# Row skewness on one core: the closing of seven blocks and the last block's row sums on GpSimd, other last pieces, five square buffers

## The chip, the cores and the metric

The kernel runs on one core of one Trainium2 chip. The metric is the device time of one execution in microseconds (us), as the median of several runs.

## The reference

```python
def reference(x):                       # x: 1024 x 8192, float32
    mean = np.mean(x, axis=-1, keepdims=True)
    std = np.std(x, axis=-1, keepdims=True)
    z = (x - mean) / (std + 1e-8)
    return np.mean(z ** 3, axis=-1).astype(np.float32)
```

It gives the skewness of each row. With the raw moments m1, m2 and m3 of a row (the means of x, x^2 and x^3), the variance is m2 - m1^2, and the result is (m3 - 3 m1 (var + m1^2/3)) var^-1.5. The kernel computes it in this form, so x is read once.

## The kernel before, in words

The 1024 rows are eight blocks of 128: row 8p + b lies in partition p of block b. A block's 8192 columns are loaded in pieces whose widths the table UNITS lists, from 4096 columns in blocks 0 and 1 down to 512 at the end of block 7 (L is 7, the last block). All loads are issued by SyncE in this order (L129) into a pool of eight x buffers; a load waits until the piece eight places earlier has been used by ScalarE, VectorE and TensorE. The schedule is manual: each engine runs its instructions in the order in which the code writes them.

Each piece goes through three engines:

- TensorE transposes it in chunks of 128 columns against the identity, all of a block's chunks accumulating into one PSUM tile `tp` (L133). At the end of a block ScalarE copies `tp` to `tsb` (L163, in the last block L139), and a matmul with a column of 1/8192 makes the row means m1 in one column of the PSUM tile `s1ps` (L164).
- ScalarE squares the piece, or slices of it where it is wide (L145), scaled so that the accumulator gives the slice's part of m2. The part goes into a column of `s2u`, K columns to a block.
- VectorE multiplies the square by x (L149), in place, and its accumulator gives the slice's part of m3 in a column of `s3u`. In this document this is "the cube" of a piece.

The squares lie in a pool of four SBUF buffers up to piece 4 of block 6, and from piece 5 of block 6 on (PSUM_FROM) in two PSUM buffers called `psq`. A square therefore waits for the cube two pieces earlier, and a cube for the square of its own piece.

After piece 2 of block 7 (EARLY_AT) the blocks 0 to 6 are closed while loads go on. ScalarE copies the seven means to `m1a` (L156), VectorE sums the K columns of every block with two reductions (L107), ScalarE makes three small tiles out of `m1a` (L112 to L114), and GpSimd does the rest in six instructions of 128 x 7, one of them a power of -1.5 (L116 to L121).

In the last block, ScalarE sums the first five parts of m2 after the fifth piece (L160). In the last piece the copy to `tsb` (L139) stands ahead of the last square. Behind it: two GpSimd additions finish m2 (L171, L172), ScalarE squares the mean (`m1sq`, L173) and makes -3 m1 (L176), GpSimd makes `var` (L174) and its power (`rr`, L175), ScalarE makes v3 = m1^2/3 + var (L177), sums all but the last part of m3 (n3, L180) and makes num = v3 (-3 m1) + n3 (L181). One VectorE instruction ends the block (L182), and one store writes all results (L186).

Of the kernel before, what the change touches and what calls it, by code (L numbers as in the profile page):

```python
# [9 lines left out]
AF = mybir.ActivationFunctionType  # L10
ALU = mybir.AluOpType
X_AXIS = mybir.AxisListType.X
# [7 lines left out]
    [2944, 2688, 2560],  # L20
    [1920, 1920, 1792, 1536, 1024],
    [1536, 1408, 1408, 1152, 1408, 1280],
    [1152, 1280, 1408, 1280, 1280, 1280, 512],
]
PSUM_FROM = (6, 5)
SUB_MAX = 2304
PS_MAX, PS_BUFS = 1536, 2
X_BUFS = 8
SQ_BUFS = 4
EARLY = 7  # L30
EARLY_AT = (7, 2)


def _slices(w, most):
# [5 lines left out]
def _plan(b, k):  # L40
    return _slices(UNITS[b][k], PS_MAX if (b, k) >= PSUM_FROM else SUB_MAX)


@with_exitstack
def kernel(
    ctx: ExitStack,
    tc: tile.TileContext,
    x: bass.AP,
    out: bass.AP,
):  # L50
    nc = tc.nc
    eng = mybir.EngineType
    ctx.enter_context(tc.manual_schedule(
        engines={eng.PE, eng.Activation, eng.DVE, eng.Pool, eng.SP}))
    P = nc.NUM_PARTITIONS
    R, C = x.shape
    NB = R // P
    L = NB - 1
    F = EARLY
    inv_n = 1.0 / float(C)  # L60
    s_scale = float(C) ** -0.5
    third = (1.0 / 3.0) ** 0.5
    assert len(UNITS) == NB and all(sum(u) == C for u in UNITS) and F == L


    xv = x.rearrange("(p b) c -> b p c", b=NB)
    ov = out.rearrange("(p b) -> p b", b=NB)


    n_sl = [sum(len(_plan(b, k)) for k in range(len(u))) for b, u in enumerate(UNITS)]  # L70
    K = max(n_sl)

    xpool = ctx.enter_context(tc.tile_pool(name="xp", bufs=X_BUFS))
    sqpool = ctx.enter_context(tc.tile_pool(name="sqp", bufs=SQ_BUFS))
    onep = ctx.enter_context(tc.tile_pool(name="onep", bufs=1))
    psq = ctx.enter_context(tc.tile_pool(name="psq", bufs=PS_BUFS, space=bass.MemoryType.PSUM))
    psum1 = ctx.enter_context(tc.tile_pool(name="ps1", bufs=1, space=bass.MemoryType.PSUM))

    def small(name, n):
        return onep.tile([P, n], FP, tag=name, name=name)  # L80

    onesn = small("onesn", 1)
    nc.vector.memset(onesn, inv_n)  # L83
    tiny = small("tiny", 1)
    nc.scalar.activation(out=tiny, in_=onesn, func=AF.Square)  # L85
    ident = small("ident", P)
    make_identity(nc, ident)
    s2u = small("s2u", NB * K)
    s3u = small("s3u", NB * K)
    nc.vector.memset(s2u, 0.0)  # L90
    nc.vector.memset(s3u, 0.0)
    junk = small("junk", K)
    expo = small("expo", F)
    nc.gpsimd.memset(expo, -1.5)
    skew = small("skew", NB)
    m1a = small("m1a", F)
    tsb = small("tsb", P)

    tp = psum1.tile([P, P], FP, tag="tp", name="tp")
    s1ps = psum1.tile([P, NB], FP, tag="s1ps", name="s1ps")  # L100
    act, g = nc.scalar.activation, nc.gpsimd

    def close_first_blocks():

        m2, m3 = small("m2a", F), small("m3a", F)
        for dst, src in ((m2, s2u), (m3, s3u)):
            nc.vector.tensor_reduce(  # L107
                out=dst, in_=src[:, 0 : F * K].rearrange("p (b c) -> p b c", c=K),
                axis=X_AXIS, op=ALU.add,
            )  # L110
        m1sq, m1sq3, nm1 = small("m1sqa", F), small("m1sq3a", F), small("nm1a", F)
        act(out=m1sq, in_=m1a, func=AF.Square)  # L112
        act(out=m1sq3, in_=m1a, func=AF.Square, scale=third)
        act(out=nm1, in_=m1a, func=AF.Copy, scale=-3.0)  # L114
        var, rr = small("vara", F), small("rra", F)
        g.tensor_tensor(out=var, in0=m2, in1=m1sq, op=ALU.subtract)  # L116
        g.tensor_tensor(out=m1sq3, in0=m1sq3, in1=var, op=ALU.add)
        g.tensor_tensor(out=m1sq3, in0=m1sq3, in1=nm1, op=ALU.mult)
        g.tensor_tensor(out=m3, in0=m3, in1=m1sq3, op=ALU.add)
        g.tensor_tensor(out=rr, in0=var, in1=expo, op=ALU.pow)  # L120
        g.tensor_tensor(out=skew[:, 0:F], in0=m3, in1=rr, op=ALU.mult)  # L121

    for b, widths in enumerate(UNITS):
        c0 = 0
        j = b * K
        for k, w in enumerate(widths):
            last_unit = b == L and k == len(widths) - 1
            xt = xpool.tile([P, w], FP, tag="x", name=f"x_{b}_{k}")
            nc.sync.dma_start(out=xt, in_=xv[b, :, c0 : c0 + w])  # L129
            c0 += w  # L130
            n = w // P
            for c in range(n):
                nc.tensor.matmul(  # L133
                    out=tp, lhsT=xt[:, c * P : (c + 1) * P], rhs=ident,
                    start=(k == 0 and c == 0), stop=(c0 == C and c == n - 1),
                    is_transpose=True,
                )
            if last_unit:
                nc.scalar.copy(out=tsb, in_=tp)  # L139
            for s, e in _plan(b, k):  # L140
                if (b, k) >= PSUM_FROM:
                    sq = psq.tile([P, PS_MAX], FP, tag="psq", name=f"psq_{b}_{k}_{s}")[:, 0 : e - s]
                else:
                    sq = sqpool.tile([P, e - s], FP, tag="sq", name=f"sq_{b}_{k}_{s}")
                act(  # L145
                    out=sq, in_=xt[:, s:e], func=AF.Square, scale=s_scale,
                    accum_out=s2u[:, j : j + 1],
                )
                nc.vector.scalar_tensor_tensor(  # L149
                    out=sq,  # L150
                    in0=sq, scalar=1.0, in1=xt[:, s:e],
                    op0=ALU.mult, op1=ALU.mult, accum_out=s3u[:, j : j + 1],
                )
                j += 1
            if (b, k) == EARLY_AT:
                nc.scalar.copy(out=m1a, in_=s1ps[:, 0:F])  # L156
                close_first_blocks()
            if b == L and k == len(widths) - 3:
                m2p = small("m2p", 1)
                act(out=junk[:, 0 : n_sl[L] - 2], in_=s2u[:, L * K : j], func=AF.Copy,  # L160
                    accum_out=m2p)
        if b < L:
            nc.scalar.copy(out=tsb, in_=tp)  # L163
        nc.tensor.matmul(out=s1ps[:, b : b + 1], lhsT=tsb, rhs=onesn, start=True, stop=True)  # L164


    p1 = s1ps[:, L : L + 1]
    m1sq, nm1, v3, m2, var, rr, num = (
        small(f"{t}_l", 1) for t in ("m1sq", "nm1", "v3", "m2", "var", "rr", "num")
    )  # L170
    g.tensor_tensor(out=m2p, in0=m2p, in1=s2u[:, j - 2 : j - 1], op=ALU.add)  # L171
    g.tensor_tensor(out=m2, in0=m2p, in1=s2u[:, j - 1 : j], op=ALU.add)  # L172
    act(out=m1sq, in_=p1, func=AF.Square)  # L173
    g.tensor_tensor(out=var, in0=m2, in1=m1sq, op=ALU.subtract)  # L174
    g.tensor_tensor(out=rr, in0=var, in1=expo[:, 0:1], op=ALU.pow)  # L175
    act(out=nm1, in_=p1, func=AF.Copy, scale=-3.0)  # L176
    act(out=v3, in_=m1sq, func=AF.Identity, scale=1.0 / 3.0, bias=var)  # L177

    n3 = small("n3_l", 1)
    act(out=junk[:, 0 : n_sl[L] - 1], in_=s3u[:, L * K : j - 1], func=AF.Copy, accum_out=n3)  # L180
    act(out=num, in_=v3, func=AF.Identity, scale=nm1, bias=n3)  # L181
    nc.vector.tensor_scalar(  # L182
        out=skew[:, L:NB], in0=s3u[:, j - 1 : j], scalar1=num, scalar2=rr,
        op0=ALU.add, op1=ALU.mult,
    )
    nc.sync.dma_start(out=ov, in_=skew)  # L186
# [30 lines left out]
```

## Time and profile before

| | |
|---|---|
| median of 10 runs | 92.0 us (91.76 to 92.26) |
| the profiled execution's own time | 91.84 us |
| its span, first to last instruction | 90.0 us |
| VectorE busy | 73.9 us (82%) |
| ScalarE busy | 69.7 us (77%) |
| TensorE matmuls busy | 66.7 us (74%) |
| GpSimd busy | 4.4 us (5%) |
| loaded from memory | 33.55 MB |
| granted TensorE clock | 0.995 |

Busy shares are means over the whole span, while the end of the kernel is a chain of small dependent steps, so the table only says which engines are in use. What the change does is read from the timeline (each instruction with start, length, engine, line and shape; in brackets the idle time before it and what ended it), from the list of waits, and from the chain of work that ended last, which goes back from the last instruction to what released each step. The times of the views count from the start of the span.

### The profile page before, as it was taken

The page shows a single profiled execution, that of the slowest core. Times are in us where ns is not written, and L with a number is a line of the kernel's source. Part 1 is how long each engine was busy: PE and PEld are TensorE (multiplying, and loading weights), DVE is VectorE, ACT ScalarE, POOL GpSimd, SP SyncE. Part 2 cuts the span into 40 slices and gives each one's busy share as a digit, 9 for nine tenths or more (in the row PEclk, how much of TensorE's full clock was granted, in tenths as well). Part 3 has the DMA queues.
Part 4 walks back from the last instruction along what each step waited for, and adds up shares of the span by engine and source line. Part 5 has one row for each costly group of instructions (what it writes and reads, how often), then busy time and mean ns, then how long its engine had stood idle before and what let it go on. Part 6 is the DMA issues. An engine that isn't in the chain of part 4 may idle for free.

```text
span 90.0 us, 1444 instructions
## 1 busy us (share of the span) xinstructions
PE 66.7 (74%) x528; PEld 60.4 (67%) x528; DVE 73.9 (82%) x90; ACT 69.7 (77%) x106; POOL 4.4 (5%) x17
## 2 busy tenths in 40 slices
PE   0003999989886959898589779889798888897800
PEld 0003999979876949687569668878687677685700
DVE  0000498969999799999988999999999989989970
ACT  6003959589894979898589889989978889799950
POOL 3000000000000000000000000000000000004640
PEclk9999999999999999999999999999999999999997
DMA  4899999999999999999999999999999999994000
GB/s 116 342 393 451 437 451 393 437 459 407 425 394 450 427 424 400 453 419 415 417 438 400 417 430 427 406 411 407 417 413 414 417 417 412 414 406 187 0 0 2
DMA packets 4614, 33.64 MB, mean 374 GB/s; under 512 B 640, under 2 KB 640, under 8 KB 3072
## 3 DMA queue, kind: packets, MB, share of 16 engines
q1 hardware_dynamic: 4608, 33.56, 89.9%
q8 instruction: 4, 0.07, 0.3%
q14 instruction: 2, 0.02, 0.0%
HBM read 33.55 MB, written 0.00 MB: 373 GB/s over the span
## 4 chain that ended last, share of the span: by engine, by line
DMA 77%; ACT 8%; SPq 4%; PE 3%; issue 2%; DVE 2%; POOL 0%; DVEq 0%; POOLq 0%; ACTq 0%
DMA x<-in_x_dram 77%; ACT sq L145 6%; SPq L129 4%; PE tp L133 3%; DVE sq L149 2%; ACT psq L145 1%; ACT num_l L181 0%; ACT v_l L177 0%; DVE skew L182 0%; POOL var_l L174 0%; ACT junk L180 0%; POOL m_l L172 0%; ACT nm_l L176 0%; ACT m1sq_l L173 0%; DVEq L182 0%
## 5 line engine op out<-in xcount | busy, mean ns | idle before, releaser
L133 PE MATMUL tp<-ident,x 128*128 128x128 f32 x512 | 64.2, 283 | 15.6 <-DMA x<-in_x_dram 15.5
L149 DVE SCALAR_TENSOR_TENSOR sq<-sq,x 128x2048 f32<-128x2048 f32 (+9 forms) x34 | 62.0, 1873 | 12.3 <-ACT sq L145 12.2
L133 PEld LDWEIGHTS tp<-ident,x 128*128 128x128 f32 x512 | 58.5, 146 | 19.9 <-DMA x<-in_x_dram 11.5
L145 ACT ACTIVATE sq<-x 128x2048 f32<-128x2048 f32 (+9 forms) x34 | 53.5, 1576 | 14.0 <-DMA x<-in_x_dram 12.0
L149 DVE SCALAR_TENSOR_TENSOR psq<-psq,x 128x1280 f32<-128x1280 f32 (+3 forms) x8 | 11.0, 1409 | 0.3 <-ACT psq L145 0.2
L145 ACT ACTIVATE psq<-x 128x1280 f32<-128x1280 f32 (+3 forms) x8 | 9.3, 1161 | 0.7 <-DMA x<-in_x_dram 0.3
L145 ACT ACTIVATION_READ_ACCUMULATOR sq<-x 128x1 f32 x34 | 6.3, 185 | 0.0
L164 PEld LDWEIGHTS s1ps<-onesn,tsb 128*128 128x128 f32 x16 | 2.4, 188 | 5.3 <-ACT tsb L163 4.7
L164 PE MATMUL s1ps<-onesn,tsb 128*128 128x1 f32 x16 | 3.1, 261 | 3.4 <-ACT tsb L163 3.0
L116 POOL TENSOR_TENSOR vara<-m2a,m1sqa 128x7 f32<-128x7 f32 x1 | 0.2, 205 | 80.6 <-DVE m3a L107 80.6
L163 ACT COPY tsb<-tp 128x128 f32<-128x128 f32 x7 | 1.7, 250 | 1.4 <-PE tp L133 1.3
L149 DVE DVE_READ_ACCUMULATOR sq<-sq,x 128x1 f32 x34 | 2.8, 82 | 0.0
L85 ACT ACT_TABLE_LOAD x1 | 1.3, 1283 | 0.7 <-PEq L201 0.7
L120 POOL TENSOR_TENSOR rra<-vara,expo 128x7 f32<-128x7 f32 x1 | 1.5, 1506 | 0.0
L145 ACT ACTIVATION_READ_ACCUMULATOR psq<-x 128x1 f32 x8 | 1.5, 187 | 0.0
L149 DVE DVE_READ_ACCUMULATOR psq<-psq,x 128x1 f32 x8 | 1.1, 141 | 0.0
L83 DVE MEMSET onesn<- 128x1 f32 x1 | 0.1, 59 | 0.8 <-PEq L201 0.8
L177 ACT ACTIVATE v_l<-m1sq_l,var_l 128x1 f32<-128x1 f32 x1 | 0.3, 294 | 0.5 <-POOL var_l L174 0.5
L182 DVE TENSOR_SCALAR skew<-s3u,num_l,rr_l 128x1 f32<-128x1 f32 x1 | 0.3, 273 | 0.5 <-ACT num_l L181 0.5
L175 POOL TENSOR_TENSOR rr_l<-var_l,expo 128x1 f32<-128x1 f32 x1 | 0.6, 560 | 0.1
L139 ACT COPY tsb<-tp 128x128 f32<-128x128 f32 x1 | 0.3, 265 | 0.2 <-PE tp L133 0.2
L181 ACT ACTIVATE num_l<-v_l,n_l,nm_l 128x1 f32<-128x1 f32 x1 | 0.4, 387 | 0.0
(29 smaller groups left out, 5.0 us busy)
## 6 DMA issues: line engine op xcount, KB each, us to landing
x<-in_x_dram SPq DMA_DIRECT2D x4, 2048.0 KB, 14.1
x<-in_x_dram SPq DMA_DIRECT2D x4, 1472.0 KB, 27.1
x<-in_x_dram SPq DMA_DIRECT2D x5, 640.0 KB, 9.3
x<-in_x_dram SPq DMA_DIRECT2D x4, 704.0 KB, 10.1
x<-in_x_dram SPq DMA_DIRECT2D x2, 960.0 KB, 19.7
x<-in_x_dram SPq DMA_DIRECT2D x2, 896.0 KB, 22.5
x<-in_x_dram SPq DMA_DIRECT2D x1, 1728.0 KB, 25.3
x<-in_x_dram SPq DMA_DIRECT2D x2, 768.0 KB, 15.2
```

The source lines that it names most:

```text
L85: nc.scalar.activation(out=tiny, in_=onesn, func=AF.Square)
L120: g.tensor_tensor(out=rr, in0=var, in1=expo, op=ALU.pow)
L129: nc.sync.dma_start(out=xt, in_=xv[b, :, c0 : c0 + w])
L133: nc.tensor.matmul(out=tp, lhsT=xt[:, c * P : (c + 1) * P], rhs=ident, start=(k == 0 and c == 0), stop=(c0 == C and c == n - 1), is_transp ...
L139: nc.scalar.copy(out=tsb, in_=tp)
L145: act(out=sq, in_=xt[:, s:e], func=AF.Square, scale=s_scale, accum_out=s2u[:, j : j + 1],)
L149: nc.vector.scalar_tensor_tensor(out=sq, in0=sq, scalar=1.0, in1=xt[:, s:e], op0=ALU.mult, op1=ALU.mult, accum_out=s3u[:, j : j + 1],)
L163: nc.scalar.copy(out=tsb, in_=tp)
L164: nc.tensor.matmul(out=s1ps[:, b : b + 1], lhsT=tsb, rhs=onesn, start=True, stop=True)
L175: g.tensor_tensor(out=rr, in0=var, in1=expo[:, 0:1], op=ALU.pow)
L177: act(out=v3, in_=m1sq, func=AF.Identity, scale=1.0 / 3.0, bias=var)
L181: act(out=num, in_=v3, func=AF.Identity, scale=nm1, bias=n3)
```

## The change

- The pool of squares in SBUF has five buffers instead of four.
- Block 7 is loaded in pieces of 1280, 1408, 1408, 1408, 1152, 896 and 640 columns.
- The closing of blocks 0 to 6 comes after piece 0 of block 7 instead of piece 2, and is done by GpSimd except for the copy `m1a`. K is 8 instead of the largest number of slices (7), and each sum over a block's 8 columns is three additions in halves: 4 + 4, 2 + 2, 1 + 1. For s2u and s3u these are six instructions; nine others follow.
- In block 7, ScalarE's partial sum of m2 is gone. GpSimd sums the seven parts in four additions after the last square in the code.
- The copy to `tsb` of block 7 stands where that of every other block stands: behind the block's last square.

```diff
-    [1152, 1280, 1408, 1280, 1280, 1280, 512],
+    [1280, 1408, 1408, 1408, 1152, 896, 640],
...
-SQ_BUFS = 4
+SQ_BUFS = 5
 EARLY = 7
-EARLY_AT = (7, 2)
+EARLY_AT = (7, 0)
...
-    K = max(n_sl)
+    K = 8
...
+    def add(out, a, b):
+        g.tensor_tensor(out=out, in0=a, in1=b, op=ALU.add)
+
     def close_first_blocks():
         m2, m3 = small("m2a", F), small("m3a", F)
         for dst, src in ((m2, s2u), (m3, s3u)):
-            nc.vector.tensor_reduce(
-                out=dst, in_=src[:, 0 : F * K].rearrange("p (b c) -> p b c", c=K),
-                axis=X_AXIS, op=ALU.add,
-            )
-        m1sq, m1sq3, nm1 = small("m1sqa", F), small("m1sq3a", F), small("nm1a", F)
-        act(out=m1sq, in_=m1a, func=AF.Square)
-        act(out=m1sq3, in_=m1a, func=AF.Square, scale=third)
-        act(out=nm1, in_=m1a, func=AF.Copy, scale=-3.0)
-        var, rr = small("vara", F), small("rra", F)
+            v = src[:, 0 : F * K].rearrange("p (b c) -> p b c", c=K)
+            add(v[:, :, 0:4], v[:, :, 0:4], v[:, :, 4:8])
+            add(v[:, :, 0:2], v[:, :, 0:2], v[:, :, 2:4])
+            add(dst, v[:, :, 0], v[:, :, 1])
+        m1sq, t, var, rr = (small(n, F) for n in ("m1sqa", "ta", "vara", "rra"))
+        g.tensor_tensor(out=m1sq, in0=m1a, in1=m1a, op=ALU.mult)
         g.tensor_tensor(out=var, in0=m2, in1=m1sq, op=ALU.subtract)
-        g.tensor_tensor(out=m1sq3, in0=m1sq3, in1=var, op=ALU.add)
-        g.tensor_tensor(out=m1sq3, in0=m1sq3, in1=nm1, op=ALU.mult)
-        g.tensor_tensor(out=m3, in0=m3, in1=m1sq3, op=ALU.add)
         g.tensor_tensor(out=rr, in0=var, in1=expo, op=ALU.pow)
+        g.tensor_scalar(out=t, in0=m1sq, scalar1=1.0 / 3.0, scalar2=None, op0=ALU.mult)
+        g.tensor_tensor(out=t, in0=t, in1=var, op=ALU.add)
+        g.tensor_scalar(out=m1a, in0=m1a, scalar1=-3.0, scalar2=None, op0=ALU.mult)
+        g.tensor_tensor(out=t, in0=t, in1=m1a, op=ALU.mult)
+        g.tensor_tensor(out=m3, in0=m3, in1=t, op=ALU.add)
         g.tensor_tensor(out=skew[:, 0:F], in0=m3, in1=rr, op=ALU.mult)
...
-            if last_unit:
-                nc.scalar.copy(out=tsb, in_=tp)
             for s, e in _plan(b, k):
...
-            if b == L and k == len(widths) - 3:
-                m2p = small("m2p", 1)
-                act(out=junk[:, 0 : n_sl[L] - 2], in_=s2u[:, L * K : j], func=AF.Copy,
-                    accum_out=m2p)
-        if b < L:
-            nc.scalar.copy(out=tsb, in_=tp)
+        nc.scalar.copy(out=tsb, in_=tp)
         nc.tensor.matmul(out=s1ps[:, b : b + 1], lhsT=tsb, rhs=onesn, start=True, stop=True)
...
-    g.tensor_tensor(out=m2p, in0=m2p, in1=s2u[:, j - 2 : j - 1], op=ALU.add)
-    g.tensor_tensor(out=m2, in0=m2p, in1=s2u[:, j - 1 : j], op=ALU.add)
+    c = s2u[:, L * K : L * K + K]
+    add(c[:, 0:3], c[:, 0:3], c[:, 3:6])
+    add(c[:, 0:1], c[:, 0:1], c[:, 1:2])
+    add(c[:, 0:1], c[:, 0:1], c[:, 2:3])
+    add(m2, c[:, 0:1], c[:, 6:7])
```

More of the change, by code (lines that the diff above doesn't have):

```diff
@@ L61 @@
     s_scale = float(C) ** -0.5
-    third = (1.0 / 3.0) ** 0.5
     assert len(UNITS) == NB and all(sum(u) == C for u in UNITS) and F == L
@@ L70 @@
     n_sl = [sum(len(_plan(b, k)) for k in range(len(u))) for b, u in enumerate(UNITS)]
-    K = max(n_sl)
+    K = 8
+    assert max(n_sl) < K and n_sl[L] == 7
     xpool = ctx.enter_context(tc.tile_pool(name="xp", bufs=X_BUFS))
@@ L126 @@
         for k, w in enumerate(widths):
-            last_unit = b == L and k == len(widths) - 1
             xt = xpool.tile([P, w], FP, tag="x", name=f"x_{b}_{k}")
```

## The prediction

> **What bounds the kernel now.** I read three views in this order: the page's DMA row, the chain of work that ended last, and the timeline of the last 15 us. The DMA row and one issue row of the page:
>
> ```profile
> DMA  4899999999999999999999999999999999994000
> ...
> x<-in_x_dram SPq DMA_DIRECT2D x1, 256.0 KB, 8.4
> ```
>
> The DMA engines are full from slice 2 to 36, and even the last and smallest piece (512 columns) is issued 8.4 us before it lands: the load queue never runs dry, so landing times are set by bytes. The end of the chain (start, length, what):
>
> ```profile
> 73.53 9.62 DMA x<-in_x_dram
> 83.15 0.04 issue
> 83.19 1.76 PE tp L133 x14
> 84.95 0.02 issue
> 84.98 0.02 ACT tsb L139
> 85.00 0.14 issue
> 85.14 0.72 ACT psq L145 x2
> 85.86 0.06 ACT m1sq_l L173
> ```
>
> So the end is last landings, then PE, then ScalarE: `tsb` (L139) stands ahead of the last square and starts 0.04 after PE ends. Now the timeline, the last landings as PE sees them (it starts some 0.04 after a landing), the hand-over between ScalarE and VectorE, and the tail:
>
> ```profile
> 75.26 1.49 DVE L149 SCALAR_TENSOR_TENSOR psq<-psq,x 128x1280 f32<-128x1280 f32 x1
> ...
> 78.49 1.42 PE L133 MATMUL tp<-ident,x 128*128 128x128 f32 x11 [0.41 <-DMA x<-in_x_dram]
> 78.53 1.35 ACT L145 ACTIVATE psq<-x 128x1408 f32<-128x1408 f32 x1 [0.32 <-DMA x<-in_x_dram]
> ...
> 80.03 1.63 DVE L149 SCALAR_TENSOR_TENSOR psq<-psq,x 128x1408 f32<-128x1408 f32 x1 [0.23 <-ACT psq L145]
> 80.07 1.31 PE L133 MATMUL tp<-ident,x 128*128 128x128 f32 x10 [0.16 <-DMA x<-in_x_dram]
> ...
> 81.64 1.31 PE L133 MATMUL tp<-ident,x 128*128 128x128 f32 x10 [0.26 <-DMA x<-in_x_dram]
> ...
> 84.98 0.27 ACT L139 COPY tsb<-tp 128x128 f32<-128x128 f32 x1 [0.22 <-PE tp L133]
> 85.14 0.61 ACT L145 ACTIVATE psq<-x 128x512 f32<-128x512 f32 x1
> ...
> 85.30 0.38 PE L164 MATMUL s1ps<-onesn,tsb 128*128 128x1 f32 x2 [0.35 <-ACT tsb L139]
> 85.67 0.19 ACT L145 ACTIVATION_READ_ACCUMULATOR psq<-x 128x1 f32 x1
> 85.76 0.16 ACT L173 ACTIVATE m1sq_l<-s1ps 128x1 f32<-128x1 f32 x1
> ...
> 86.27 0.19 POOL L174 TENSOR_TENSOR var_l<-m_l,m1sq_l 128x1 f32<-128x1 f32 x1
> 86.50 0.29 ACT L177 ACTIVATE v_l<-m1sq_l,var_l 128x1 f32<-128x1 f32 x1 [0.51 <-POOL var_l L174]
> 87.49 0.27 DVE L182 TENSOR_SCALAR skew<-s3u,num_l,rr_l 128x1 f32<-128x1 f32 x1 [0.50 <-ACT num_l L181]
> ```
>
> What is to be seen: the transposed sum and the last square run at the same time today (PE has the sum at 85.68 while ScalarE squares until 85.75), and the square, not the sum, holds the row sum back.
>
> **What the Trainium skill says.** "PSUM — Partial Sum Buffer", section "Engine vs sequencer instructions": the ScalarE, VectorE and GpSimdE queues are strict FIFO, so a copy written behind a square can't pass it. The trace agrees: every ScalarE row comes in program order. "SBUF — State Buffer", section "Who interferes with whom": a VectorE instruction with two SBUF inputs contends with a GpSimd one that reads SBUF, one with a single SBUF input does not. The cubes of block 7 take psq from PSUM, and the trace agrees: a 1280 cube is followed by the next after 1.41 us with GpSimd idle (75.26 to 76.67) and after 1.41 with four GpSimd additions over it (81.81 to 83.22). "Perfetto Trace Analysis", section "GPSIMD Engine Instruction": go by start-to-start spacing, not by reported spans. Here the 7-element additions show 0.20 each and stand 0.28 apart; I use 0.28.
>
> **The change part by part.**
>
> *Five square buffers.* They end ScalarE's waits for VectorE in SBUF (1.7 us in four waits in the list of waits). The last is ahead of piece 4 of block 6, and gains 0.04. VectorE is back to back there and the loads are full anyway; nothing at the end. Cost nothing.
>
> *Closing on GpSimd, after piece 0 of block 7.* Gone are two VectorE reductions (81.58 to 81.81, 0.23), three ScalarE ones (80.08 to 80.39, 0.31) and the partial sum L160 (0.24). Added on GpSimd: 15 instructions, of them one power (1.51, from its row; 1.58 apart). The 28- and 14-element additions have no row; the page "GPSIMD Engine Reference", section 3.1, gives some 2.6 cycles an element, at 1.2 GHz an estimate of 0.05 for 21 elements more, so 0.33 is my value. Bounds: 0.28 (no element cost) and 1.5 (as dear as the power). s2u's three start by 75.2, s3u's follow the last cube of block 6 at 76.8; 76.8 + 3 x 0.33 + 8 x 0.28 + 1.58 = 81.6. Nothing asks for GpSimd before the last block's sums at 84.8: 3.2 us of cover. The copy `m1a` needs PE's sum of block 6 (75.86) and runs at 76.6, in ScalarE's wait for piece 1.
>
> *Last block in pieces 1280, 1408, 1408, 1408, 1152, 896, 640.* Landings: PE's starts 78.49, 80.07, 81.64 are 1280 columns apart, 1.575 each, or 1.23 ns a column; columns landed by then are 3840, 5120, 6400. So the new ends land at: piece 0 75.3, piece 1 (2688) 77.0, piece 2 (4096) 78.76, piece 3 (5504) 80.50, piece 4 (6656) 81.91, piece 5 by 83.0, piece 6 by 83.8. Hand-over times from the rows: a 1408 square's start to its cube's start 1.50 (78.53 to 80.03); cube start to next cube 1.55 for 1408, 1.41 for 1280, 1.32 for 1152 (76.67 to its accumulator read at 77.99); cube start to the square that reuses its PSUM buffer, two pieces on, 0.17 more (1.73 for 1408, 80.03 to 81.76; 1.49 for 1152). Interpolated between the 512 and 1408 rows, a square's accumulator read begins after 0.86 for 896 columns and 0.64 for 640, and a cube takes 1.04 for 896. With A for a square's start and D for a cube's:
> A2 = 78.76 + 0.05 = 78.81, D2 = 80.31. A3 = 80.55 (landing), D3 = 82.05 (D2 + 1.55 = 81.86 is earlier). D4 = D3 + 1.55 = 83.60. A5 = D3 + 1.73 = 83.78. D5 = D4 + 1.32 = 84.92. A6 = D4 + 1.49 = 85.09, today 85.14. The saved 0.23 of VectorE is thus spent on waiting for the larger pieces 1 to 3, and the last square starts where it did. Its accumulator read begins at 85.73.
>
> *`tsb` behind the last square, which the short description does not name.* PE is done by 84.6 (12 matmuls at 0.125 from piece 5's landing), but ScalarE reaches the copy only at 85.73 + 0.10 = 85.83, not 84.98. From copy to PE's end 0.70 (84.98 to 85.68), 0.04 to wake ScalarE: `m1sq` at 86.57, not 85.76. Then 0.16 for it and 0.06 for GpSimd to wake: `var` at 86.8 instead of 86.27. From there all rows are as before: 0.23 to v3, 0.99 to the last VectorE row: 88.02 against 87.49, **+0.53**.
>
> *Row sums of the last block on GpSimd.* Three additions wait for square 5 (read by 84.83) and are through by 85.7; the fourth waits for square 6 (85.92), starts at about 86.0 and ends at 86.2. That is 0.6 ahead of `var`'s other input: nothing. If GpSimd is late by more, the excess is added whole, since `var` and the power stand behind it. The power (87.07 to 87.63), the last cube (ends 86.9) and n3's inputs stay ahead of 88.02.
>
> Sum: +0.53. The profiled execution took 91.84 (span 90.0, 1.84 outside it), so its like would take 92.37; the median of ten is 92.0, 0.16 above it, hence 92.5.
>
> **The rivals.**
> *GpSimd late (slower still).* If the wide additions cost near 1.5, four of them add 4.7: the closing ends at 86.3, the four sums at 87.4 against 86.8: about +0.6 more, 93.1. For it: 4 such shapes have no row, and bigger operands made the power 1.51 instead of 0.56. Against: additions of 7 and of 1 element differ by 0.01.
> *Loads earlier (faster).* Piece 3's landing sets D3 to D6. If earlier buffer releases or larger pieces brought it forward by 0.87 or more, the cubes would run back to back from 75.26 (+ 1.41 + 1.41 + 3 x 1.55 = D4 at 82.73), and the end would come at 88.02 - 0.87 = 87.15: 0.34 before today's, 91.65. It decides from a landing 0.53 earlier on. For it: ScalarE runs ahead more freely. Against: DMA full, the same bytes, the queue 8 us deep.
> *No change that can be measured* (within 0.2%, 0.18 us, about what a measurement of this kernel can tell from no change): the same with 0.35 to 0.7 of it, 92.0. For it: wait times in a tail differ by some 0.1. Against: the 0.81 on the copy is program order.
>
> **How the numbers follow.** Forecast as worked out 0.75, within 92.3 to 92.75 since each of some five hand-overs is known to about 0.05; GpSimd late 0.12; no change 0.07; faster 0.06. Slower by over 0.2%: 0.87. Range 92.2 to 92.85: it leaves out faster, no change and the half of the late case.
>
> **What would show it.** Right: `tsb` on ScalarE behind the last square and 0.8 later; the last square within 0.1 of 85.14; `var` waiting for ScalarE's `m1sq`, not for a GpSimd sum; closing done by 82; VectorE waiting for squares in pieces 1 to 3; last row at 88.0. Wrong: `var` waiting behind GpSimd's own additions, or piece 3 landing before 80.

## The result and the profile after

The changed kernel takes **92.57 us** (median of 9 runs, 92.44 to 92.73) against 92.02 (32 runs): ratio 1.0060, 95% interval 1.0051 to 1.0069, slower by 0.55 us. 92.5 was forecast, slower with a chance of 0.87.

The profiled execution took 92.79 us, its span is 91.0. It is 0.22 above its kernel's median, where the profiled one of before was 0.18 below: 0.40 of the 0.95 between the two profiles is the choice of execution. It is seen in the loads. Piece 5 of block 6, to which the change does nothing, lets TensorE start at 74.09 instead of 73.76; in the traces of e1, e7 and e8 below, which are the same as the changed kernel up to there, the start is at 73.81 to 73.85. Where a time below is called *aligned*, this 0.33 is taken off.

From the DMA view of the changed kernel, the DMA row and the issue row of the last and smallest piece (now 640 columns):

```profile
DMA  4899999999999999999999999999999999991000
...
x<-in_x_dram SPq DMA_DIRECT2D x1, 320.0 KB, 8.3
```

The DMA engines are as full as before, and the last piece is again issued more than 8 us before it lands. The end of the chain of work that ended last (start, length, what):

```profile
85.45 0.03 ACT psq L144
85.47 0.62 issue
86.09 0.19 ACT psq L144
86.28 0.16 ACT tsb L157
86.44 0.04 issue
86.48 0.40 PE s1ps L158 x2
86.88 0.02 issue
86.90 0.17 ACT m1sq_l L170
```

Before, the copy to `tsb` stood between TensorE and the last square, and `m1sq` came right behind the square's accumulator read. Now the square comes first, then its read, then the copy, then the matmul, and only then `m1sq`: all in a row, where before the matmul ran beside the square. The timeline of the changed kernel:

```profile
78.95 1.63 DVE L148 SCALAR_TENSOR_TENSOR psq<-psq,x 128x1408 f32<-128x1408 f32 x1 [0.34 <-ACT psq L144]
...
80.68 1.63 DVE L148 SCALAR_TENSOR_TENSOR psq<-psq,x 128x1408 f32<-128x1408 f32 x1
...
80.87 4.04 PE L134 MATMUL tp<-ident,x 128*128 128x128 f32 x32 [0.31 <-DMA x<-in_x_dram]
...
82.41 1.63 DVE L148 SCALAR_TENSOR_TENSOR psq<-psq,x 128x1408 f32<-128x1408 f32 x1
...
85.45 0.71 ACT L144 ACTIVATE psq<-x 128x640 f32<-128x640 f32 x1 [0.27 <-DVE psq L148]
...
86.19 0.25 ACT L157 COPY tsb<-tp 128x128 f32<-128x128 f32 x1
...
86.42 0.19 POOL L104 TENSOR_TENSOR m_l<-s2u 128x1 f32<-128x1 f32 x1 [0.43 <-ACT tsb L157]
...
86.90 0.17 ACT L170 ACTIVATE m1sq_l<-s1ps 128x1 f32<-128x1 f32 x1 [0.47 <-PE s1ps L158]
...
87.22 0.19 POOL L171 TENSOR_TENSOR var_l<-m_l,m1sq_l 128x1 f32<-128x1 f32 x1 [0.60 <-ACT nm_l L173]
...
88.44 0.27 DVE L179 TENSOR_SCALAR skew<-s3u,num_l,rr_l 128x1 f32<-128x1 f32 x1 [1.20 <-ACT num_l L178]
```

To be read here: the sum in `tp` is ready at 84.91 (80.87 + 4.04), and the copy starts at 86.19, 1.28 later, while ScalarE is at the square of piece 5 until 85.18, waits 0.27 for VectorE to free a PSUM buffer, and then squares piece 6. The last m2 addition on GpSimd starts at 86.42 and ends at 86.61, long before `var` (87.22): the row sums on GpSimd are not what `var` waits for. VectorE waits for the wider pieces: the cubes of pieces 1, 2 and 3 start 1.73 apart (78.95, 80.68, 82.41), where the next one follows after 1.55 (83.96).

### The profile page after: what moved, and what is told of

Its sections match the earlier page's. It is cut to its first block, busy times and chain, and to the rows that moved or that the text cites. A ratio compares the mean times of both kernels' runs of the same rounds, so it can differ in the third digit from the quotient of the medians.

```text
span 91.0 us, 1445 instructions
## 1 busy us (share of the span) xinstructions
PE 66.8 (73%) x528; PEld 60.5 (67%) x528; DVE 73.7 (81%) x88; ACT 69.3 (76%) x101; POOL 6.8 (7%) x28
## 4 chain that ended last, share of the span: by engine, by line
DMA 67%; issue 9%; ACT 9%; DVE 8%; SPq 3%; PE 0%; POOL 0%; DVEq 0%; ACTq 0%
DMA x<-in_x_dram 67%; DVE sq L148 6%; ACT sq L144 6%; SPq L130 3%; ACT psq L144 2%; DVE psq L148 2%; PE s1ps L158 0%; ACT num_l L178 0%; ACT v_l L174 0%; DVE skew L179 0%; POOL var_l L171 0%; ACT junk L177 0%; ACT m1sq_l L170 0%; ACT tsb L157 0%; ACT nm_l L173 0%
## 5 line engine op out<-in xcount | busy, mean ns | idle before, releaser
L148 DVE SCALAR_TENSOR_TENSOR psq<-psq,x 128x1408 f32<-128x1408 f32 (+4 forms) x8 | 11.0, 1412 | 0.4 <-ACT psq L144 0.3
L144 ACT ACTIVATE psq<-x 128x1408 f32<-128x1408 f32 (+4 forms) x8 | 9.3, 1163 | 1.7 <-DMA x<-in_x_dram 0.9
L104 POOL TENSOR_TENSOR s2u<-s2u 128x1 f32<-128x1 f32 (+3 forms) x5 | 1.1, 211 | 78.0 <-ACT psq L144 77.8
L172 POOL TENSOR_TENSOR rr_l<-var_l,expo 128x1 f32<-128x1 f32 x1 | 0.6, 582 | 0.1
L104 POOL TENSOR_TENSOR s3u<-s3u 128x28 f32<-128x28 f32 (+1 forms) x2 | 0.5, 228 | 1.0 <-DVE psq L148 0.9
```

What stands on the lines that cost most here:

```text
L104: g.tensor_tensor(out=out, in0=a, in1=b, op=ALU.add)
L144: act(out=sq, in_=xt[:, s:e], func=AF.Square, scale=s_scale, accum_out=s2u[:, j : j + 1],)
L148: nc.vector.scalar_tensor_tensor(out=sq, in0=sq, scalar=1.0, in1=xt[:, s:e], op0=ALU.mult, op1=ALU.mult, accum_out=s3u[:, j : j + 1],)
```

## The experiments

All ratios are to the kernel before on the same chip, with 95% intervals. The runs are from several chips, on which the kernel before has medians from 91.92 to 92.02, so kernels are compared by their ratios.

| kernel | median us | ratio |
|---|---|---|
| changed kernel | 92.57 | 1.0060 (1.0051 to 1.0069) |
| e1: changed, copy ahead of the last square | 92.01 | 1.0009 (0.9997 to 1.0021) |
| e2: before, copy behind the last square | 92.20 | 1.0025 (1.0017 to 1.0034) |
| e3: before, five buffers | 91.97 | 1.0007 (0.9997 to 1.0018) |
| e4: before, new pieces | 92.16 | 1.0023 (1.0015 to 1.0030) |
| e5: before, closing on GpSimd | 91.92 | 1.0005 (0.9995 to 1.0014) |
| e6: before, row sums on GpSimd | 91.89 | 1.0001 (0.9994 to 1.0009) |
| e11: before, new pieces and copy behind | 92.67 | 1.0072 (1.0059 to 1.0084) |
| e8: changed, closing behind piece 4 | 93.81 | 1.0204 (1.0191 to 1.0217) |
| e9: changed, all squares in SBUF | 94.83 | 1.0317 (1.0297 to 1.0337) |
| e7: e1, last square in SBUF | 92.36 | 1.0039 (1.0025 to 1.0053) |
| e10: e1, three PSUM buffers, 1024-column pieces | 91.86 | 0.9982 (0.9974 to 0.9990) |
| e12: e10, copy behind the last square | 91.93 | 0.9999 (0.9990 to 1.0007) |

**e1, the copy's place undone.**

```diff
+            if b == L and k == len(widths) - 1:
+                nc.scalar.copy(out=tsb, in_=tp)
             for s, e in _plan(b, k):
...
-        nc.scalar.copy(out=tsb, in_=tp)
+        if b < L:
+            nc.scalar.copy(out=tsb, in_=tp)
```

> The changed kernel with one thing undone: in block 7 the copy to tsb stands ahead of the last square again. Theory (the copy behind the last square puts the matmul and m1sq on the path): m1sq comes right behind the last square's accumulator read, var at the pace of the last m2 addition, 0.54 earlier than in the changed kernel (87.22 there): 92.57 - 0.54 = 92.03 us, level with the kernel before. Rival A (GpSimd's row sums or closing hold the end): no gain, 92.5 to 92.6. Rival B (later landings of the larger pieces hold the end whatever stands on ScalarE): 92.4 to 92.6.

Measured 92.01, the theory's number: everything else of the change together can't be told from no change, and is at most 0.2%. The timeline of e1:

```profile
84.83 0.25 ACT L140 COPY tsb<-tp 128x128 f32<-128x128 f32 x1
...
85.93 0.15 ACT L173 ACTIVATE m1sq_l<-s1ps 128x1 f32<-128x1 f32 x1
...
86.43 0.19 POOL L174 TENSOR_TENSOR var_l<-m_l,m1sq_l 128x1 f32<-128x1 f32 x1
```

The copy starts at 84.83 instead of 86.19, `m1sq` at 85.93 directly behind the last square, and `var` comes at 86.43. In the changed kernel it was 87.22. The cube of piece 4 starts at 83.70 here and at 83.96 there, so 0.26 of the 0.79 between them is the loads, and 0.53 the copy's place. Both rivals fall.

**e2, e4 and e11: the copy's place and the pieces, alone and together, on the kernel before.**

```diff
-            if last_unit:
-                nc.scalar.copy(out=tsb, in_=tp)
...
-        if b < L:
-            nc.scalar.copy(out=tsb, in_=tp)
+        nc.scalar.copy(out=tsb, in_=tp)
```

is e2; e4 is the line of widths alone,

```diff
-    [1152, 1280, 1408, 1280, 1280, 1280, 512],
+    [1280, 1408, 1408, 1408, 1152, 896, 640],
```

and e11 is both.

> The kernel before with one thing of the change: the copy to tsb of block 7 behind the last square. There the last square (512 columns) stood behind the copy and can now start at 84.84 (the PSUM buffer of piece 4's cube) instead of 85.14, its read at 85.37, the copy at 85.46, m1sq at 86.20, var at 86.43 against 86.27. Theory (the position costs what is not won back by the earlier square): +0.16, 92.18 us. Rival A (the copy's position costs its full 0.53 whatever the pieces are): 92.55. Rival B (it costs nothing, the pieces or GpSimd do): 92.0.

> The kernel before with the new widths of block 7 only (the copy ahead of the last square, closing on VectorE and ScalarE as before). Theory: the small ScalarE closing steps delay square 3 to 80.7 and the two reductions stand behind cube 2, so cube 3 starts at 82.2, cube 4 at 83.75, the last square at 85.24 and var at 86.48 instead of 86.27: +0.2, 92.2 us. Rival A (pieces alone make the whole loss): 92.5. Rival B (pieces alone cost nothing): 92.0.

> The kernel before with two things of the change: the new widths of block 7 and the copy to tsb behind the last square (closing as before on VectorE, ScalarE and GpSimd). Alone they cost 0.2 each. Theory (with the wide pieces the last square can't start earlier when the copy is moved away, since it waits for cube 4's PSUM buffer at 85.24, so the copy's delay comes whole): read of the last square at 85.88, copy at 85.97, m1sq at 86.71, var at 87.0 against 86.27: +0.7, 92.7 us. Rival (the two costs only add): +0.4, 92.4 us.

Measured 92.20, 92.16 and 92.67; the theories had 92.18, 92.2 and 92.7. Alone, each costs 0.25% and 0.23%. Together they cost 0.72%, and not the 0.48% of a mere sum. The last square, in the timeline of e2,

```profile
84.92 0.60 ACT L143 ACTIVATE psq<-x 128x512 f32<-128x512 f32 x1
```

and in that of e11:

```profile
85.31 0.71 ACT L143 ACTIVATE psq<-x 128x640 f32<-128x640 f32 x1 [0.27 <-DVE psq L147]
```

With the old pieces the last square started at 85.14, behind the copy; with the copy gone from ahead of it, it starts at 84.92 in e2, as soon as the PSUM buffer of cube 4 is free (84.88), and so gives back part of the delay. With the new pieces that buffer comes free later, and the square waits for it in either case: until 85.31 in e11, where the bracket names VectorE, and until 85.23 in e4, though the copy is over at 85.10 there (84.86 + 0.24). The accumulator read of cube 4 ends at 85.19 in e4. Its timeline, the copy and the last square:

```profile
84.86 0.24 ACT L139 COPY tsb<-tp 128x128 f32<-128x128 f32 x1
...
85.23 0.71 ACT L145 ACTIVATE psq<-x 128x640 f32<-128x640 f32 x1
```

So nothing comes back when the copy is moved away.

**e3, e5 and e6: the three other parts, each alone on the kernel before.**

```diff
-SQ_BUFS = 4
+SQ_BUFS = 5
```

is e3. e5 takes the new `close_first_blocks` with EARLY_AT (7, 0) and K = 8, and e6 the four additions in place of L160, L171 and L172, both as the diff of the change has them.

> The kernel before with five SBUF buffers for squares. Theory (loads are full, VectorE is back to back where ScalarE waited): 92.0 us, within 0.1. Rival (buffers release x earlier and the load stream ends earlier, or the stream is disturbed): a time outside 91.9 to 92.15, with landings in block 7 moved by as much.

> The kernel before with the closing of blocks 0 to 6 as GpSimd instructions after piece 0 of block 7, K 8, everything else as before (pieces, tsb ahead of the last square, ScalarE's partial sum of m2). Theory: VectorE saves 0.23 and ScalarE 0.3, but the last square waits for the copy to tsb, and that for TensorE at 84.94, as before: 92.0 us, within 0.1. Rival A (GpSimd's closing slows VectorE or comes late): 92.2 or more. Rival B (the freed 0.23 reaches the end): 91.8.

> The kernel before with only the row sums of the last block as four GpSimd additions (L160's partial sum on ScalarE gone). Theory: the first three lie under the last two squares, the fourth waits for the last square as the addition before did: 92.0 us, within 0.1. Rival A (four additions in a row come late, each 0.28): up to 92.5. Rival B (ScalarE freed by 0.24 starts the squares earlier and gains): 91.8.

Measured 91.97, 91.92 and 91.89, each with 1 inside its interval. The copy to `tsb` in the timeline of e5:

```profile
84.90 0.27 ACT L141 COPY tsb<-tp 128x128 f32<-128x128 f32 x1 [0.27 <-PE tp L135]
```

It still waits for TensorE, and the last square stands behind it, so what VectorE and ScalarE save has nowhere to go, as the theory said. In e3 the fifth buffer wins ScalarE no time: its waits for VectorE among the SBUF squares (1.7 us in four in the kernel before) are gone from the list of waits, but those for VectorE and for loads together come to 14.0 us, against 13.7 before, and the idle times ahead of pieces 2 and 4 of block 6 are still 0.27 and 0.47, now ended by a landing. In the changed kernel's own list the waits for VectorE still stand, with 1.9 us in five.

**e8, GpSimd made late.**

```diff
-EARLY_AT = (7, 0)
+EARLY_AT = (7, 4)
```

> The changed kernel with the closing behind piece 4 of block 7 (the copy m1a comes at 83.6, so GpSimd's eight instructions behind it, 3.64 us in the changed kernel's trace, end at 87.4 instead of 81.66, and the four row sums follow). Theory (GpSimd is off the path in the changed kernel only because of its cover; when late, the excess is added whole): last row sum at 88.2, var at 88.5 instead of 87.22: +1.3, 93.9 us. Rival (row sums are already on the path in the changed kernel): the whole 5.7 us of shift appears, 98 us. Rival (GpSimd plays no part): 92.6.

Measured 93.81. The timeline of e8:

```profile
86.97 0.20 POOL L123 TENSOR_TENSOR skew<-m3a,rra 128x7 f32<-128x7 f32 x1
...
87.94 0.19 POOL L104 TENSOR_TENSOR m_l<-s2u 128x1 f32<-128x1 f32 x1
88.21 0.19 POOL L171 TENSOR_TENSOR var_l<-m_l,m1sq_l 128x1 f32<-128x1 f32 x1
```

Here the closing's last instruction runs at 86.97, and the last addition and `var` stand behind it on GpSimd without idle time. So the prediction's rival "GpSimd late" is a real mechanism with the price it was given, excess added whole; the changed kernel escapes it by its cover.

**e9, all squares in SBUF.**

```diff
-PSUM_FROM = (6, 5)
+PSUM_FROM = (8, 0)
```

> The changed kernel with all squares in SBUF (five buffers) and none in PSUM. Two things change: cubes have two SBUF inputs while GpSimd adds, and the last square no longer waits for the PSUM buffer of cube 4. Theory A (no contention to speak of, the PSUM buffer holds the last square, and with it the copy to tsb): last square at 84.4 instead of 85.45, var 1.05 earlier, end 1.0 earlier: 91.5 to 91.6 us. Theory B (as the Trainium skill's SBUF page says, GpSimd's reads contend with such cubes): cubes of pieces 0 to 3 over GpSimd's closing are longer than the 1.41 and 1.55 us of a free VectorE, and part of the gain is lost: 91.7 to 93.

Measured 94.83, above both expectations. The last square did start early (84.11), as theory A had it, and it did not matter. The contention of theory B is there, but not where I put it. The timeline of e9:

```profile
77.01 1.34 POOL L104 TENSOR_TENSOR m2a<-s2u 128x7 f32<-128x7 f32 x1
...
80.40 1.65 POOL L104 TENSOR_TENSOR m3a<-s3u 128x7 f32<-128x7 f32 x1
...
82.01 0.20 POOL L115 TENSOR_TENSOR m1sqa<-m1a 128x7 f32<-128x7 f32 x1
...
82.08 1.63 DVE L148 SCALAR_TENSOR_TENSOR sq<-sq,x 128x1408 f32<-128x1408 f32 x1
82.29 1.49 POOL L116 TENSOR_TENSOR vara<-m2a,m1sqa 128x7 f32<-128x7 f32 x1
```

`m2a` and `m3a` are additions of 7 elements (to a partition), which take 0.21 and 0.20 in the changed kernel; here their rows are 1.34 and 1.65 long. `m1sqa`, which starts at 82.01 in the gap between two cubes, takes 0.20, and the next one, of the same size, takes 1.49 and ends at 83.78, when the cube of 82.08 is over (83.71). The cubes hardly suffer: 1.63 for 1408 columns, as in the changed kernel. So VectorE keeps what it has and GpSimd waits for the end of the cube. The closing ends at 88.21 instead of 81.66, and the row sums come late as in e8.

**e7, only the last square in SBUF** (on e1), to take away its wait for cube 4 and to test e9's reading on one instruction.

```diff
-                if (b, k) >= PSUM_FROM:
+                if (b, k) >= PSUM_FROM and (b, k) != (7, 6):
```

> e1 (the changed kernel with the copy to tsb ahead of the last square), with the last square in SBUF, so that it does not wait for cube 4. Theory A (no contention): last square, m1sq and m2 0.2 earlier, 91.8 us. Theory B (a GpSimd addition that comes up while a cube with two SBUF inputs runs waits for that cube's end, as in e9): the last cube (from 86.1 to about 86.9) now has two SBUF inputs, and var stands behind it, at 86.9 instead of 86.43: 92.4 to 92.5 us.

Measured 92.36, next to theory B's 92.4 and far from theory A's 91.8. The timeline of e7:

```profile
86.08 0.82 DVE L150 SCALAR_TENSOR_TENSOR sq<-sq,x 128x640 f32<-128x640 f32 x1
86.23 0.72 POOL L174 TENSOR_TENSOR var_l<-m_l,m1sq_l 128x1 f32<-128x1 f32 x1
```

The square came 0.2 earlier, but `var` of one element, 0.19 long in e1, comes up 0.15 into a cube with two SBUF inputs and ends with it (86.95 against 86.90).

**e10 and e12, a version against the tail's own limits.** e10, on e1:

```diff
-    [1280, 1408, 1408, 1408, 1152, 896, 640],
+    [1024, 1024, 1024, 1024, 1024, 1024, 1024, 640, 384],
...
-PSUM_FROM = (6, 5)
+PSUM_FROM = (7, 0)
...
-PS_MAX, PS_BUFS = 1536, 2
+PS_MAX, PS_BUFS = 1024, 3
...
-    add(m2, c[:, 0:1], c[:, 6:7])
+    add(c[:, 0:1], c[:, 0:1], c[:, 6:7])
+    add(c[:, 0:1], c[:, 0:1], c[:, 7:8])
+    add(m2, c[:, 0:1], c[:, 8:9])
```

s2u and s3u get one more column for the ninth piece.

> e1 with block 7 in pieces of 1024 x 7, 640 and 384 columns, its squares in three PSUM buffers of 1024 columns in place of two of 1536 (piece 5 of block 6 in SBUF), and two more row-sum additions. Theory (the tail is the last landing plus one hand-over for each engine; two buffers of wide pieces make the last square wait for a cube two pieces back): squares start at their landings, the last one at about 84.3, m1sq at 85.1, var at 85.4, n3 behind cube 7 at 86.2, last row near 87.0 instead of 88.44 in the changed kernel: 91.1 to 91.3 us. Rival (more pieces cost VectorE and ScalarE as much as the hand-over saves, or landings hold the end): 91.9 to 92.2.

Measured 91.86, ratio 0.9982 with an interval below 1: faster than both kernels, but than the kernel before by only some 0.15 us where I expected 0.8. The squares of pieces 3 to 6 do start at their landings, 0.03 to 0.04 after TensorE. What I had wrong is TensorE. Its timeline from piece 6's landing on:

```profile
82.93 1.97 PE L134 MATMUL tp<-ident,x 128*128 128x128 f32 x16
```

It has the 16 matmuls of the last three pieces to do, 0.123 each, and never waits among them: piece 6 alone keeps it until 83.9. It ends at 84.90, and an earlier landing of the last two pieces would not change that. The expectation had the last square at about 84.3, so the copy and TensorE's sum ahead of that. The copy starts at 84.98, and the last square behind it at 85.15.

> e10 (1024-column pieces, three PSUM buffers) with the copy to tsb behind the last square, as the changed kernel has it. In e10's trace ScalarE is free and the buffer is free at 84.76, while TensorE's sum ends at 84.9 and the copy starts at 84.98. Theory (the position costs only what the earlier start of the last square does not give back): last square 84.76, its read 85.18, copy 85.27, m1sq 86.0, var 86.3 against 86.17: +0.1 to e10, 91.95 us. Rival (the copy behind the last square costs half a microsecond wherever it stands): 92.4 us.

e12 is e10 with the copy behind the last square. Measured 91.93, ratio 0.9999; the theory had 91.95, the rival 92.4. Its timeline:

```profile
84.53 0.47 ACT L144 ACTIVATE psq<-x 128x384 f32<-128x384 f32 x1
...
85.03 0.24 ACT L157 COPY tsb<-tp 128x128 f32<-128x128 f32 x1
```

TensorE is done at 84.68 here. Where ScalarE can start the last square before that (84.53), the same order that costs the changed kernel 0.5 us costs 0.16, the difference of the two ratios (give or take 0.1, by their intervals). The two traces give 0.11, with `var` counted from TensorE's start on piece 6: 3.35 behind it in e12 (82.71 to 86.06), 3.24 in e10 (82.93 to 86.17).

## Why the prediction was right

- *The copy behind the last square* was named as the cause of the whole loss, and e1 shows it: undoing it takes away all that can be measured. It has this price only with the new pieces, as the next point says. Aligned, the copy was predicted at 85.83 and is at 85.86, `m1sq` at 86.57 and is at 86.57.
- *The last square starts where it did* (85.09 predicted, 85.12 aligned). This was needed for the full price, as e2 and e11 show: with the old pieces the copy's place costs 0.25%, with the new ones the two cost 0.72%.
- *VectorE's saved time is spent on waiting for wider pieces.* e4 has the pieces' price alone (0.23%). What the freed VectorE gives back lies in the step from e11 to the changed kernel, 1.0072 to 1.0060, about 0.1 us; the sums with the rows of before had put the last square at 85.24 with the old closing and at 85.09 with the new. The intervals of the two ratios overlap, but the traces show it. With each trace shifted so that TensorE starts on piece 5 of block 6 at 73.76, the last square is at 85.24 and 85.25 with the old closing (e4, e11) and at 85.11 and 85.12 with the new (e1, the changed kernel).
- *Landings.* Predicted for pieces 1 to 4: 77.0, 78.76, 80.50, 81.91. Measured, aligned and 0.04 ahead of TensorE: 77.04, 78.77, 80.50, 81.90. The rival of earlier loads has nothing in the trace: as profiled, every one of these landings is later than predicted.
- *Five buffers, the closing and the row sums cost nothing:* e3, e5, e6. The reason given for the buffers was wrong in part: ending ScalarE's 1.7 us of waits for VectorE wins no time; in e3 landings end the same idle times. The closing ended at 81.33 aligned (81.6 predicted); a wide addition and the instruction behind it start 0.29 to 0.34 apart, where 0.33 was estimated.
- *Mis-sized, by little:* the step from `m1sq` to `var`. I gave GpSimd 0.06 to wake after `m1sq`; it starts 0.15 after it (87.07 to 87.22), 0.08 after the end of `nm_l`, which stands behind `m1sq` on ScalarE. So `var` is at 86.89 aligned instead of 86.8, and the last row at 88.11 instead of 88.02. The two profiles thus differ by 0.62 aligned, and the medians by 0.55. That the forecast's 0.53 met the medians to 0.02 is in part luck, since it was the sum for the profiles. A wait for `nm_l` is not needed to explain the 0.15: in e10, GpSimd's sum behind the last but one square starts 0.14 after that square's read (84.84 to 84.98), and no other instruction of ScalarE ends between. In the kernel before, too, the last m2 addition starts 0.15 after the last square's read (85.86 to 86.01), which the prediction could have used.
- *GpSimd late* did not happen here, and e8 priced it: with the closing's end 5.5 us later in its trace (87.17 against 81.66) the end moves by 1.3 (the difference of the two ratios).

## What to carry to other kernels

In a tail of single small steps, look for two chains that run side by side on different engines and meet in one instruction: an engine's program order can put one behind the other, and its price is what the earlier start of the instruction now in front doesn't give back. Before such a reorder is judged free, ask what else holds that instruction; here a PSUM buffer filled two pieces back did, and the new widths of the same change had made it come free later. And where GpSimd has small steps on the path, try to keep one operand of a busy VectorE out of SBUF: in e9 and e7 such steps cost 0.2 us alone and up to the length of a whole cube behind one.

## What was not expected of the hardware

With two SBUF inputs on VectorE the contention falls nearly all on one side in e9: three 7-element GpSimd instructions went from 0.2 to between 1.3 and 1.7 us, while a 1408-column cube stayed at 1.63. The Trainium skill, "SBUF — State Buffer", section "Who interferes with whom", says that such instructions contend and that issue order decides who blocks. The traces agree: the GpSimd steps named here all came up after a cube had started and ended within 0.1 us of its end, and the one cube of e9 that was held up, by 0.08 us (1.57 for 1280 columns against 1.49 for the next), started at 75.28, just behind a GpSimd addition at 75.26. The second point is that the load stream does not end at full rate: in the kernel before, the mean busy share of the 16 DMA engines is 0.80 from 81 to 82 us, 0.28 from 82 to 83 and 0.09 from 83 to 83.5, while TensorE still waits for a landing at 83.15. Whether some engines end before others or all slow down, the view doesn't show.
